# MLA attention: the queries' norm ahead of the up projection, first keys inside the queries' down projection, probabilities scaled on ScalarE

## The chip, the cores and the metric

One core of a Trainium2 chip runs the whole program. The metric is the device time of one execution in microseconds, the median of the runs shown; lower is better. The engines are named as in the profile: PE is TensorE's matrix multiplication (PEld its weight loads), DVE is VectorE, ACT is ScalarE, POOL is GpSimd, SP is the queue that issues most DMAs.

## The reference

The program is one step of a two-layer streaming encoder: a GLA layer and then an MLA layer, each between two half-step SwiGLU blocks, for 528 prompt rows (16 meta tokens and 512 frames) and 32 sample rows. The change lies in the MLA mixer:

```
def rmsnorm(x, w):
    y = x32 * lax.rsqrt(jnp.mean(x32 * x32, axis=-1, keepdims=True) + RMS_EPS)
    return (y * w.astype(jnp.float32)).astype(x.dtype)
...
cq, ckv, kr = jnp.split(xn @ w_down, [MLA_Q_RANK, MLA_Q_RANK + MLA_KV_RANK], axis=-1)   # 384, 256, 64
q = (rmsnorm(cq, q_norm) @ w_uq).reshape(B, L, MLA_HEADS, MLA_NOPE + MLA_ROPE)          # 8 heads, 128 + 64
q_rope = apply_rope(q[..., MLA_NOPE:], pos)
ckv = rmsnorm(ckv, kv_norm)
kr = apply_rope(kr[:, :, None, :], pos)[:, :, 0]
...
p = jax.nn.softmax(jnp.where(mask, s, -jnp.inf), axis=-1)      # per block of 128 queries
o = jnp.einsum('blhr,rhv->blhv', o_lat, w_uv).reshape(B, L, MLA_HEADS * MLA_V)
return o @ w_out, ckv, kr
```

The norm's factor, one number per row, commutes with the up projection `w_uq`; it may be multiplied in before or after it.

## The kernel before

All activations lie transposed: channels on the 128 partitions, rows along the free dimension (544 query columns: 512 frames and 32 sample rows; in two halves of 272, `HALF_Q`). Precision comes from splitting each fp32 operand into an upper part and a remainder: `split` writes the upper part with an ACT copy (line 374) and the remainder with a DVE subtraction (line 375), and every product is three matmuls, upper by upper (418), upper by weight remainder (419), remainder by upper (421) in `mm`, or 425 to 427 in `mm3`. Weights come in by DMA from SP (`load`, two raw buffers `raw`), and are split too (`whi`, `wlo`). PSUM holds three banks `ps` for projections and five banks `s` for scores, transposes and norms in this stage.

Code is written in pieces; a scheduler of the recording layer sets the order in which instructions stand in each engine's queue from the pieces' order and its own costs. Each engine then works off its queue strictly in order.

In `mla` the latent and rotary keys are projected first. Then come the queries: three blocks of 128 channels (`cq`) for the first half of columns, then three for the second half, each block 24 matmuls on `x`. Each block is multiplied by the input's norm (DVE, line 1158), by the norm's weights, and split (`cqh`, `cql`, lines 1160 and 1161); its squares are summed for the queries' own norm (`square`). `roots` sums the squares over partitions (three matmuls, line 450) and takes the inverse square root on DVE in three rounds of small operations (lines 485 to 493, tiles `rv`, `ry`, `rt`); its `finish` spreads the result over the partitions with three transposes (line 457). `query_norm` puts it into `yq` (line 1144) and scales cosine and sine by it on POOL (line 1146), so that the rotary part of the queries carries the norm without a further step; the plain part gets it after the up projection (line 1216), and is then split.

In `attention`, `keys(h)` makes a head's keys in two halves of 264 columns, `values(pr)` a head pair's values in five pieces, `queries(pr)` a pair's queries in six pieces: rotary, plain, plain for each half of the columns (nine matmuls each on `cqh`, `cql`; the rotary piece has four ACT copies, line 1013, a POOL product, line 1015, and four DVE steps behind it). `scores(h, t)` makes the scores of 128 queries against 144, 272, 400 or 528 keys and calls `softmax`: maximum on DVE (1027, 1030), exponential with a running sum on ACT (1032), reciprocal (1036) and scaling of the probabilities `p` (1038) on DVE. `transposes` turns the probabilities over on TensorE and splits them, `weigh` multiplies by the values. `weave(main, fill)` puts pieces of other work between the steps of a head. The order at the start was

```
for f in keys(0) + query_norm[:1] + keys(1) + query_norm[1:] + v0[:2] + queries(0):
    f()
weave([partial(scores, 0, t) for t in range(4)], v0[2:] + queries(1))
```

where `query_norm` holds `query_roots` and `query_norm` of the second half; those of the first half are called within the down projection of the second.

## Time and profile before

| | before |
|---|---|
| median of 3 runs | 2039.81 us (2038.86 to 2039.95) |
| profiled execution: time, span | 2041.99 us, 2040.2 us |
| granted TensorE clock, mean | 0.995 |
| PE, PEld busy | 2006.2 us (98%), 1976.2 us (97%) |
| DVE, ACT, POOL busy | 1603.3 us (79%), 1003.8 us (49%), 52.5 us (3%) |
| queries' down projection to the last head | about 1447 to 1630 us of the span |

The span runs from the first to the last instruction; the time also holds what lies around it. A busy share is an average over stages: what a change in one stage is worth is read from that stage, from what its engines wait for. A wait is put down to the release that came last. Matmuls overlap, so a group's mean duration is longer than the distance from one to the next.

### The profile page before, as it was taken

What the parts mean: (1) busy time and instruction counts of PE and PEld (TensorE: products, weight loads), DVE (VectorE), ACT (ScalarE), POOL (GpSimd) and SP (SyncE); (2) the same over time, 40 slices, a digit from 0 to 9 for tenths busy, and PEclk for the clock granted to TensorE, in tenths of its full rate; (3) what the DMA queues carried; (4) which work ended last, traced back from release to release, by engine and by line L of the source; (5) the groups of instructions that cost most, each with busy time, mean ns of one, the idle gap of its engine ahead of it and who ended that gap; (6) DMA issues with size and microseconds to landing.
All of it is one profiled execution on the core that took longest, in us unless ns stands there. A gap on an engine that the chain in (4) does not pass through costs nothing.

```text
span 2040.2 us, 38174 instructions
## 1 busy us (share of the span) xinstructions
PE 2006.2 (98%) x15408; PEld 1976.2 (97%) x15408; DVE 1603.3 (79%) x3046; ACT 1003.8 (49%) x1821; POOL 52.5 (3%) x121
## 2 busy tenths in 40 slices
PE   9999999999999999999999999999989999999997
PEld 8999999989999999999999999999989999999997
DVE  7778788556657988788888878786798898887884
ACT  6444445455535544444555444454476565444451
POOL 0000000101110000000000000000110000000000
PEclk9999999999999999999999999999999999999999
DMA  5232322212223132323313322323111413333221
GB/s 182 73 106 87 109 84 81 80 60 70 68 83 114 63 105 77 102 91 109 104 50 100 105 94 94 99 67 104 62 52 48 145 34 104 102 94 109 84 74 64
DMA packets 91904, 180.16 MB, mean 88 GB/s; under 512 B 10240, under 2 KB 21888, under 8 KB 91728
## 3 DMA queue, kind: packets, MB, share of 16 engines
q1 hardware_dynamic: 86688, 171.91, 26.6%
q10 hardware_dynamic: 5040, 5.82, 0.9%
q8 instruction: 121, 1.98, 0.4%
q14 instruction: 55, 0.45, 0.1%
HBM read 173.69 MB, written 3.99 MB: 87 GB/s over the span
## 4 chain that ended last, share of the span: by engine, by line
PE 81%; DVE 12%; ACT 3%; DMA 2%; issue 1%; POOL 0%; SPq 0%; DVEq 0%; ACTq 0%; POOLq 0%
PE Y L421 8%; PE Y L418 8%; PE Y L419 8%; PE A L418 5%; PE A L419 5%; PE A L421 5%; PE ps L418 4%; PE ps L421 4%; PE ps L419 3%; DVE wlo L375 3%; PE B L419 3%; PE B L421 3%; PE B L418 3%; PE C L421 3%; PE C L419 3%; PE C L418 3%
## 5 line engine op out<-in xcount | busy, mean ns | idle before, releaser
L418 PE MATMUL Y<-ah,whi 128*128 128x280 f32 (+1 forms) x1408 | 372.7, 291 | 3.2 <-ACT ah L374 2.4
L419 PE MATMUL Y<-ah,wlo 128*128 128x280 f32 (+1 forms) x1408 | 371.7, 290 | 0.0
L375 DVE TENSOR_TENSOR wlo<-fr,whi 128x1024 fp32r<-128x1024 f32 (+1 forms) x297 | 357.8, 1214 | 11.3 <-ACT whi L374 10.6
L374 ACT CAST whi<-fr 128x1024 fp32r<-128x1024 f32 (+1 forms) x297 | 308.5, 1048 | 103.4 <-PE C L421 39.6
L418 PE MATMUL A<-x,whi 128*128 128x280 f32 (+1 forms) x1056 | 281.8, 292 | 5.4 <-ACT whi L374 3.7
L419 PE MATMUL A<-x,wlo 128*128 128x280 f32 (+1 forms) x1056 | 281.2, 292 | 0.1
L418 PEld LDWEIGHTS Y<-ah,whi 128*128 128x128 f32 x1408 | 264.6, 188 | 4.5 <-ACT ah L374 3.3
L419 PEld LDWEIGHTS Y<-ah,wlo 128*128 128x128 f32 x1408 | 265.3, 188 | 0.0
L655 DVE SCALAR_TENSOR_TENSOR h<-Y,h 128x280 f32<-128x280 f32 (+1 forms) x320 | 141.1, 444 | 156.3 <-PE Y L421 155.8
L375 DVE TENSOR_TENSOR wlo<-raw,whi 128x512 fp32r<-128x512 f32 (+5 forms) x231 | 196.0, 850 | 78.9 <-ACT whi L374 74.1
L374 ACT CAST whi<-raw 128x512 fp32r<-128x512 f32 (+5 forms) x231 | 169.7, 736 | 163.4 <-PE ps L421 46.2
L421 PE MATMUL Y<-al,whi 128*128 128x280 f32 (+1 forms) x1408 | 232.7, 290 | 0.0
L293 DVE TENSOR_TENSOR fr<-fr 128x1024 f32<-128x1024 f32 x160 | 195.1, 1219 | 18.3 <-DMA fr<-W 15.7
L418 PEld LDWEIGHTS A<-x,whi 128*128 128x128 f32 x1056 | 199.9, 189 | 6.2 <-ACT whi L374 4.0
L419 PEld LDWEIGHTS A<-x,wlo 128*128 128x128 f32 x1056 | 199.9, 189 | 0.4 <-DVE wlo L375 0.4
L421 PEld LDWEIGHTS Y<-al,whi 128*128 128x128 f32 x1408 | 199.2, 188 | 0.0
L419 PE MATMUL B<-x,wlo 128*128 128x280 f32 (+1 forms) x704 | 186.4, 291 | 0.5 <-DVE wlo L375 0.5
L418 PE MATMUL B<-x,whi 128*128 128x280 f32 (+1 forms) x704 | 186.6, 291 | 0.0
L421 PE MATMUL A<-x,whi 128*128 128x280 f32 (+1 forms) x1056 | 178.9, 291 | 0.0
L418 PE MATMUL C<-x,whi 128*128 128x280 f32 (+1 forms) x672 | 177.5, 290 | 0.0
L419 PE MATMUL C<-x,wlo 128*128 128x280 f32 (+1 forms) x672 | 177.5, 290 | 0.0
L520 ACT COPY r<-A 128x560 f32<-128x560 f32 (+1 forms) x120 | 74.8, 623 | 159.2 <-PE A L421 158.4
(405 smaller groups left out, 4112.8 us busy)
## 6 DMA issues: line engine op xcount, KB each, us to landing
fr<-W SPq DMA_DIRECT2D x352, 256.0 KB, 3.4
raw<-W SPq DMA_DIRECT2D x80, 512.0 KB, 3.5
raw<-W SPq DMA_DIRECT2D x100, 256.0 KB, 2.9
raw<-W SPq DMA_DIRECT2D x40, 128.0 KB, 2.1
raw<-W SPq DMA_DIRECT2D x4, 384.0 KB, 3.1
h<-xT SPq DMA_DIRECT2D x2, 560.0 KB, 8.2
o_y<-h SPq DMA_DIRECT2D x8, 136.0 KB, 2.5
o_y<-h ACTq DMA_DIRECT2D x8, 136.0 KB, 2.3
```

Source lines behind the costliest of these rows:

```text
L293: self.net.nc.vector.tensor_tensor(r[out], r[x], r[y], op=ALU.add)
L374: self.nc.scalar.copy(hi, src)
L375: self.nc.vector.tensor_tensor(lo, src, hi.bitcast(F32), op=ALU.subtract)
L418: f(hi[:, b0 + k, :], xh[:, c], start=not more and k == 0, stop=False)
L419: f(lo[:, b0 + k, :], xh[:, c], start=False, stop=False)
L421: f(hi[:, b0 + k, :], xl[:, c], start=False, stop=k == n - 1)
L520: nc.scalar.copy(r[:, :, :n], of[:, :, :n])
L655: nc.vector.scalar_tensor_tensor(self.h[:, m, c], Y[:, :n], 0.5, self.h[:, m, c], op0=ALU.mult, op1=ALU.add)
```

## The change

The norm of the queries is multiplied in ahead of the up projection: `query_norm` reads the spread roots from PSUM, multiplies the three blocks of a half by them and by the weights (three DVE operations, line 1145 of the new code), and then splits all three blocks at once (a cast and a subtraction of 3 x 272 columns). The copies into `yq`, the scaling of cosine and sine and the sixteen products after the up projection go, and so do the scaled copy and the subtraction of each block (six of each); the plain pieces split their PSUM bank directly. The up projection of a half can now start only after that half's norm.

`keys` becomes a method, and the two halves of head 0's keys are put between the down projection's pieces for the second half of columns. Then come the first three pieces of head 0's and 1's queries, half of head 1's keys, the second half's norm, and the weave of head 0's scores with the remaining queries, keys and values. The pool of the down projection (`brief`) is closed after the norms, and the pool `at` (probabilities, values) is opened after that; its eight memsets on POOL move with it.

The scaling of the probabilities goes from a DVE operation to an ACT copy with a per-partition scale, 34 of them.

```
-        nc.vector.tensor_scalar(p[:, :n], p[:, :n], st[:, 5:6], None, op0=ALU.mult)
+        nc.scalar.activation(p[:, :n], p[:, :n], AF.Copy, scale=st[:, 5:6])
...
                 def query_norm(hf):
                     c = slice(*HALF_Q[hf])
-                    nc.scalar.copy(yq[:, c], norms.pop(hf)())
-                    for t in (self.cos, self.sin):
-                        nc.gpsimd.tensor_tensor(t[:, c], t[:, c], yq[:, c], op=ALU.mult)
+                    y = norms.pop(hf)()
+                    for m in range(3):
+                        nc.vector.scalar_tensor_tensor(cq[:, m, c], cq[:, m, c], nv[:, wq + m:wq + m + 1], y,
+                                                       op0=ALU.mult, op1=ALU.mult)
+                    self.split(cqh[:, :, c], cql[:, :, c], cq[:, :, c])
...
+                kt = {}
+                k0 = self.keys(two, kt, kph, kpl, 0)
                 for hf, (c0, c1) in enumerate(HALF_Q):
...
                         nc.vector.tensor_tensor(cq[:, m, c0:c1], Y[:, :n], xs.y[:, c0:c1], op=ALU.mult)
-                        w = nv[:, wq + m:wq + m + 1]
-                        nc.scalar.activation(cqh[:, m, c0:c1], cq[:, m, c0:c1], AF.Copy, scale=w)
-                        nc.vector.scalar_tensor_tensor(cql[:, m, c0:c1], cq[:, m, c0:c1], w,
-                                                       cqh[:, m, c0:c1].bitcast(F32), op0=ALU.mult, op1=ALU.subtract)
                         self.square(cq[:, m, c0:c1], n, hf, m == 0)
+                        if hf == 1 and m < 2:
+                            k0[m]()
...
-                qf = self.temp(("vh", "t")[j])
-                nc.vector.tensor_tensor(qf[:, :n], Y[:, :n], yq[:, c], op=ALU.mult)
-                self.split(q[h][0][:, c], q[h][1][:, c], qf[:, :n])
+                self.split(q[h][0][:, c], q[h][1][:, c], Y[:, :n])
...
+        q0, k1 = queries(0), keys(1)
+        for f in query_norm[:1] + q0[:3] + k1[:1] + query_norm[1:]:
+            f()
+        brief.close()
+        at = gone("at")
...
         v0 = values(0)
-        for f in keys(0) + query_norm[:1] + keys(1) + query_norm[1:] + v0[:2] + queries(0):
-            f()
-        weave([partial(scores, 0, t) for t in range(4)], v0[2:] + queries(1))
+        weave([partial(scores, 0, t) for t in range(4)], q0[3:] + k1[1:] + v0 + queries(1))
```

Three places in the engines' queues show what moved. First TensorE's queue around the transposes of the second half's norm (line 457; `ry` holds the roots, `cqh` and `cql` the parts of the queries' latent, `whi` and `wlo` those of a weight). Before, they stand within an up-projection piece:

```order
L419 MATMUL ps<-cqh,wlo 128x272
L421 MATMUL ps<-cql,whi 128x272
L457 MATMUL s<-ident,ry 128x128 x3
L421 MATMUL ps<-cql,whi 128x272 x2
L418 MATMUL ps<-cqh,whi 128x272
```

Now (`kpl` is the remainder of the latent keys, `kh` and `kl` are head 0's keys, `rph` and `rpl` the rotary keys, `x` here the queries):

```order
L421 MATMUL ps<-kpl,whi 128x264 x2
L457 MATMUL s<-ident,ry 128x128 x3
L425 MATMUL s<-kh,x 128x144
L426 MATMUL s<-kh,x 128x144
L427 MATMUL s<-kl,x 128x144
L1341 MATMUL s<-rph,x 128x144
L1342 MATMUL s<-rpl,x 128x144
```

The transposes moved from among the up projections to between head 1's first keys and head 0's first scores; the up projections of the second half stand behind those scores.

Second, VectorE's queue from the second half's sum of squares on (`rv`, `ry`, `rt` are the roots' small tiles; `acc`, `y`, `sq` belong to the rotary piece, `wlo` to a weight). Now:

```order
L485 TENSOR_SCALAR rv<-s 128x3
L486 TENSOR_SCALAR ry<-rv 128x3
L491 TENSOR_TENSOR rt<-ry 128x3
L1014 TENSOR_TENSOR acc<-ps,cos 128x272
L492 TENSOR_TENSOR rt<-rt,rv 128x3
L1017 TENSOR_TENSOR y<-acc,sq 64x272
L493 SCALAR_TENSOR_TENSOR ry<-rt,ry 128x3
L375 TENSOR_TENSOR wlo<-raw,whi 128x512
L491 TENSOR_TENSOR rt<-ry 128x3
L1018 TENSOR_TENSOR sq<-acc,sq 64x272
L492 TENSOR_TENSOR rt<-rt,rv 128x3
L1210 TENSOR_TENSOR x<-y,x 64x272
```

The rotary steps of the first queries moved in between the rounds of the root; before, splits of keys, values and weights stood there.

Third, ScalarE's queue at the load of the exponential's table (line 1032). Before:

```order
L374 CAST x<-t 128x272
L1207 CAST x<-sq 64x272
L374 CAST vh<-ps 128x256 x2
L1032 ACT_TABLE_LOAD
L1032 ACTIVATE p_17441,st<-s,st 128x144
```

Now:

```order
L374 CAST cqh<-cq 128x3x272
L1013 COPY sq<-ps 32x272
L1032 ACT_TABLE_LOAD
L1032 ACTIVATE p_17567,st<-s,st 128x144
L1013 COPY sq<-ps 32x272
L1038 ACTIVATE p_17567<-p_17567,st 128x144
L1013 COPY sq<-ps 32x272 x2
L374 CAST x<-ps 128x272 x2
```

The load and the first exponential moved in among the copies of the second half's rotary piece, ahead of the casts of that half's plain queries, and the scaling of the probabilities is new in this queue.

## The prediction

> **What bounds the kernel now.** I read the page's totals first, then the chain, then busy time by stretch in the MLA stage, then TensorE's own waits there.

> ```profile
> span 2040.2 us, 38174 instructions
> PE 2006.2 (98%) x15408; PEld 1976.2 (97%) x15408; DVE 1603.3 (79%) x3046; ACT 1003.8 (49%) x1821; POOL 52.5 (3%) x121
> PE 81%; DVE 12%; ACT 3%; DMA 2%; issue 1%; POOL 0%; SPq 0%; DVEq 0%; ACTq 0%; POOLq 0%
> ```

> TensorE is busy 98% of the span and carries 81% of the chain. The change removes no matmul, so it can only move TensorE's idle time, and only in the MLA stage. The view by stretch (span times, then busy time of each engine, clock last but two) shows where that idle time lies:

> ```profile
> core 0: us, PE busy (x) PEld busy (x) DVE busy (x) ACT busy (x) POOL busy (x), PEclk, DMA share, GB/s
> 1462.00:1476.00 14.00, 13.99 (x113) 13.55 (x112) 11.39 (x33) 8.12 (x21) 4.77 (x12) 1.00 0.28 82
> 1476.00:1494.00 18.00, 16.08 (x124) 15.43 (x122) 16.49 (x48) 14.12 (x36) 4.85 (x10) 1.00 0.21 63
> 1494.00:1510.00 16.00, 14.12 (x102) 12.84 (x101) 15.50 (x50) 11.95 (x33) 3.01 (x8) 1.00 0.03 9
> 1510.00:1530.00 20.00, 18.27 (x131) 16.57 (x130) 18.70 (x62) 15.85 (x47) 1.72 (x5) 1.00 0.23 66
> 1530.00:1562.00 32.00, 32.00 (x246) 31.06 (x246) 27.51 (x93) 19.16 (x61) 0.67 (x4) 1.00 0.24 73
> 1562.00:1600.00 38.00, 36.05 (x269) 34.53 (x267) 35.14 (x100) 26.12 (x68) 3.86 (x10) 1.00 0.26 77
> 1600.00:1645.00 45.00, 45.00 (x346) 43.98 (x346) 34.79 (x90) 22.43 (x52) 0.00 (x0) 1.00 0.35 115
> ```

> Length less PE busy gives 1.92, 1.88, 1.73, 0, 1.95 and 0 us from 1476 on: 7.5 us, 0.37% of the span, is all that there is to win. The stretches with idle time are those in which VectorE is busy 92 to 97%; at 86% (1530 to 1562) there is none. The longest waits name the same engine:

> ```profile
> PE ps L418 <- DVE vl L375: 1.8, 1, 1.8
> PE ps L418 <- DVE st L1030: 1.4, 1, 1.4
> PE s L425 <- DVE pTl L375: 0.9, 1, 0.9
> PE s L1274 <- ACT vh L374: 0.8, 1, 0.8
> ```

> **The change part by part.** Four places, walked through in TensorE's new order. These rows set the clock of the walk (start, duration, what):

> ```profile
> 1458.84 0.72 PE L450 MATMUL s<-ones,acc 128*128 128x1 f32 x6
> 1462.51 0.49 PE L457 MATMUL s<-ident,ry 128*128 128x128 f32 x3
> 1465.84 0.38 PE L1166 MATMUL s<-ident,cn 128*32 128x128 f32 x2
> 1466.79 0.29 PE L418 MATMUL ps<-kph,whi 128*128 128x264 f32 x1
> 1467.53 0.28 PE L418 MATMUL ps<-kph,whi 128*128 128x264 f32 x1
> 1468.38 0.80 PE L450 MATMUL s<-ones,acc 128*128 128x1 f32 x6
> 1469.21 0.16 DVE L485 TENSOR_SCALAR rv<-s 128x3 f32<-128x3 f32 x1 [0.30 <-PE s L450]
> 1473.57 0.51 PE L457 MATMUL s<-ident,ry 128*128 128x128 f32 x3
> 1474.17 0.29 PE L418 MATMUL ps<-cqh,whi 128*128 128x272 f32 x1
> 1475.31 0.29 PE L418 MATMUL ps<-cqh,whi 128*128 128x272 f32 x1
> ```

> Half a head's keys take 0.74 us (1466.79 to 1467.53), nine matmuls of a query piece 1.14 (1474.17 to 1475.31), roots plus one piece of the down projection 3.67 (1458.84 to 1462.51), transposes plus the next piece 3.33 (1462.51 to 1465.84). The rest comes from groups (busy us, mean ns of one, idle before):

> ```profile
> L1102 DVE SCALAR_TENSOR_TENSOR cn<-ck,nv,s 128x280 f32<-128x280 f32 x4 | 1.9, 504 | 0.0
> L375 DVE TENSOR_TENSOR kl<-ps,kh 128x264 fp32r<-128x264 f32 x16 | 6.6, 419 | 0.0
> L375 DVE TENSOR_TENSOR wlo<-raw,whi 128x768 fp32r<-128x768 f32 x4 | 3.8, 944 | 0.0
> L1216 DVE TENSOR_TENSOR vh<-ps,yn 128x272 f32<-128x272 f32 x8 | 3.4, 428 | 0.0
> L1038 DVE TENSOR_SCALAR p<-p,st 128x144 f32<-128x144 f32 (+3 forms) x32 | 12.5, 390 | 0.4
> L374 ACT CAST whi<-raw 128x1024 fp32r<-128x1024 f32 x12 | 12.6, 1051 | 4.1 <-PE ps L421 3.1 <-PE ps L426 0.8
> L1160 ACT ACTIVATE cqh<-cq,nv 128x272 fp32r<-128x272 f32 x6 | 3.1, 523 | 2.4 <-DVE cq L1158 2.4
> L1013 ACT COPY sq<-ps 32x272 f32<-32x272 f32 x32 | 12.1, 378 | 1.3 <-PE ps L421 0.8
> L1032 ACT ACTIVATE p<-s,st 128x144 f32<-128x144 f32 x8 | 3.1, 384 | 1.4 <-DVE st L1030 1.2
> L1032 ACT ACTIVATE p<-s,st 128x400 f32<-128x400 f32 x8 | 4.7, 593 | 4.2 <-DVE st L1030 4.2
> L1032 ACT ACT_TABLE_LOAD x1 | 1.3, 1283 | 0.0
> ```

> *First half's norm.* Head 0's keys (two halves) now stand between the pieces of the down projection, so TensorE has 0.74 + 3.09 us between roots and transposes and 0.74 + 3.08 between transposes and the first up projection. In the second gap stand VectorE's three multiplies (3 x 0.50), ScalarE's cast of 816 columns (0.87, scaled from 1.05 for 1024) and VectorE's subtraction of 816 (1.0, scaled from 0.94 for 768) with some 1.8 us of other work: the upper part is ready in time, the lower is needed only after six matmuls. Cost 0; without the keys as cover the lower part would come about 0.7 late (0.25 + 0.43 + 1.5 + 1.8 + 1.0, of which some 0.3 overlaps, against 3.08 + 0.14 + 0.75). The loads of the query weights go ahead of those of head 1's keys and the values on SP's queue; each piece still lands a buffer's turn before its split, cost 0. GpSimd's four scalings of cosine and sine go; its eight memsets now follow the first rotary product and are over before the first values are split, cost 0.

> *Second half's norm (a).* TensorE reaches the second transposes at 1458.84 + 3.67 + 0.74 + 3.33 + 0.74 + 0.14 + 3 x 1.14 + 0.62 (roots) + 0.74 = 1472.2. Its roots stand 0.74 + 13/9 x 1.14 + 0.62 ahead of that, at 1469.2; VectorE answers 0.83 us later, as at 1468.38 and 1469.21. There the square root's chain took 4.36 us up to the transposes (1469.21 to 1473.57) with six other operations in between. Now eight stand in between (seven of about 0.43, one of some 0.69, together 3.7 against 3.2): 4.9. The transposes start at 1474.9: a wait of 2.7 us where nine up-projection matmuls used to cover it. Between 0.3 (chain undisturbed) and 3.5 (rotary steps late).

> *Behind it (b, c).* Ten score matmuls (1.2 us) follow the transposes; meanwhile VectorE needs 0.25 + 3 x 0.50 and ScalarE 0.87 before the half-1 up projection may start: 0.3 + 2.6 - 1.5 gives b = 1.4. The lower part comes 1.0 after the cast, needed after six matmuls (0.75): c = 0.25.

> *Scores behind it (d).* Scores of queries 256 to 383 need the half-1 piece of head 0's queries, split by ScalarE behind a rotary copy (0.38), the table load (1.28), the first exponential (0.38), a copy, the first new scaling (0.42), two copies (0.76) and the cast itself (0.4): 4.0 us after the rotary piece, and 0.2 to begin. TensorE has 2.3 us of other up projection: d = 1.9, against 0.6 if the load fell into idle time. On the old queue the load stood behind value casts, with the scores not yet done.

> [...]

> ```profile
> 588.37 1.28 ACT L842 ACT_TABLE_LOAD   x1
> 589.66 0.67 ACT L842 ACTIVATE ab<-ab 128x560 f32<-128x560 f32 x1
> ```

> *ScalarE late with the next pair (e).* From the cast on ScalarE has some 9.8 us of queue before it frees the banks of the next pair's queries, TensorE 11.8 to get there; whether it also waits for TensorE on the way decides. Between 0 and 1.8 (the longest bank wait in the waits above); I take 1.0, the middle.

> *Probabilities and queries.* VectorE loses 34 scalings (0.39 each, 13 us) and 16 multiplies (0.43 each, 6.9). ScalarE gains 34 scalings. None like it is in the trace on p; 0.523 for 272 columns with a per-partition scale, and the exponentials' slope (0.209 over 256 columns), give 0.42 to 0.73, mean 0.575: 19.6 us. By stretch from 1494 (4, 6, 8 and 9 scalings, 4, 3, 0 and 4 multiplies) VectorE falls to 78, 76, 76 and 79%, ScalarE rises to 89, 96, 74 and 82%. Reading the idle time off today's stretches by the busier engine (86%: none; 92.5%: 5% of the stretch; 93.5%: 9%; 97%: 12%): 0.4, 2.1, 0 and 0, so 2.5 remain of 5.6. Ends 0 and 5.6.

> *Sum.* New waits 2.7 + 1.4 + 0.25 + 1.9 + 1.0 = 7.25, remaining 2.5, less the old 7.5: +2.25 us on a span of 2040.2. The profiled execution took 1.8 us beside its span and 2.2 more than the median of the three runs, 2039.81. Forecast: 2042.1, 0.1% longer. No change within 0.2% (4.1 us), about what a measurement of this kernel can tell, is 2035.7 to 2043.9.

> **The rivals.** *Faster.* The chain of the root runs undisturbed (a = 0.3 to 0.5), the table load falls into ScalarE's idle time (d = 0.6), and with VectorE below 80% no old wait survives: 0.5 + 1.4 + 0.25 + 0.6 - 7.5 = -4.75, 2035.1. For it speaks that at 86% VectorE costs nothing; against it that the eight operations and the load stand in the queues in that order. It needs a + d below about 1.7.

> *Slower: ScalarE takes VectorE's place.* From 1494 to 1530 its queue is 89 and 96% full, and each scaling waits in it for VectorE's reciprocal with casts behind it that free TensorE's banks. If the old 5.6 stays, the sum is 7.25 + 5.6 - 7.5 = +5.4, 2045.2. It decides from 4.4 us of remaining idle time on. For it: ScalarE's share there reaches what costs VectorE 9 to 12% today. Against: after 1530 it has a quarter free. [...]

> *No effect because the waits merely change place* is the forecast itself.

> **How the numbers follow.** Forecast case within 0.2%: 0.55, since a, b and d follow from fixed queues and they about equal what is saved. Slower 0.29: any 1.8 us more than my sum, from e or ScalarE's stretch. Faster 0.16. The low end, 2036.0, lets go some 0.15; the high end, 2046.5, is the forecast with the slower rival's 5.6 and a at 3.5 (2046.0), half a microsecond added; beyond it some 0.05.

> **What would show it.** Right: TensorE stops of 2 to 3 us ahead of the second query norm's transposes, 1 to 2 ahead of the half-1 up projection, about 2 ahead of the scores on ScalarE's cast of queries, and after them fewer waits on VectorE; ScalarE at 90% or more from 1494 to 1530. Wrong: transposes without a wait, or the total idle time from 1476 to 1645 below 4 or above 12 us.

## The result and the profile after

The changed kernel took 2053.16 us (median of 4 runs, 2048.41 to 2054.78) against 2039.88 of the kernel before beside it: ratio 1.0058, 95% interval 1.0046 to 1.0070. It is slower, by about 12 us as the ratio has it and 13.3 between the two medians; the forecast was 2042.1 with 2036.0 to 2046.5. The profiled execution took 2052.83 us with a span of 2051.0, 10.8 more than the span of before.

The page's totals of the kernel after:

```profile
span 2051.0 us, 38132 instructions
PE 2012.3 (98%) x15408; PEld 1982.7 (97%) x15408; DVE 1588.6 (77%) x2998; ACT 1017.0 (50%) x1849; POOL 49.0 (2%) x117
```

The same 15408 matmuls, and yet TensorE is busy 6.1 us longer. To place it, the next rows cut all kernels at the same two matmuls, one in the FFN ahead of the MLA stage (the 10501st) and one towards the stage's end (the 3150th from the last), so that the stretch holds the same work each time. Columns as in the view by stretch shown before; this is the kernel before:

```profile
1387.58:1629.56 241.98, 232.72 (x1761) 224.39 (x1759) 197.56 (x589) 142.20 (x371) 20.54 (x50) 1.00 0.25 80
```

And the kernel after:

```profile
1388.32:1637.22 248.90, 235.82 (x1760) 227.04 (x1758) 183.03 (x541) 155.59 (x399) 17.02 (x46) 0.99 0.24 78
```

The stage is 6.92 us longer. Length less PE busy is the idle time: 13.08 against 9.26, so 3.82 more. The other 3.10 is busy time above 232.72: the same matmuls at a granted clock that was not always 1.00 (0.99 in the mean here, last column but two). From here on "idle" and "clock price" of a kernel mean these two numbers, taken from its own row. VectorE lost 14.5 us of work and ScalarE gained 13.4, as the change wants, and it did not help.

Of the rest, 0.74 lies ahead of the stretch, 0.19 in the 340 us behind it, and 2.99 in the tail, whose code the change does not touch. The tail before and after, from the same matmul to the end:

```profile
1969.86:2040.20 70.34, 57.74 (x452) 56.23 (x450) 37.62 (x88) 16.55 (x30) 0.00 (x0) 0.95 0.25 77
```

```profile
1977.71:2051.04 73.33, 59.60 (x452) 57.99 (x450) 38.05 (x88) 16.55 (x30) 0.00 (x0) 0.91 0.24 74
```

Of that, 1.86 is busy time again, at a lower clock (PEclk 0.95 and 0.91); the other 1.13 is idle time. So 4.96 of TensorE's 6.1 us are found. By stretch within the stage, the kernel after:

```profile
core 0: us, PE busy (x) PEld busy (x) DVE busy (x) ACT busy (x) POOL busy (x), PEclk, DMA share, GB/s
1462.00:1476.00 14.00, 11.64 (x93) 11.23 (x91) 11.62 (x37) 7.22 (x17) 1.25 (x5) 1.00 0.22 68
1476.00:1494.00 18.00, 14.88 (x92) 14.02 (x93) 11.48 (x34) 10.09 (x25) 3.99 (x11) 0.81 0.07 22
1494.00:1510.00 16.00, 14.39 (x109) 13.45 (x108) 13.04 (x39) 14.62 (x41) 3.06 (x8) 1.00 0.18 59
1510.00:1530.00 20.00, 19.78 (x140) 18.69 (x141) 16.79 (x54) 18.20 (x50) 2.85 (x6) 1.00 0.16 47
1530.00:1562.00 32.00, 30.54 (x235) 29.46 (x235) 26.41 (x87) 23.73 (x71) 0.67 (x4) 1.00 0.24 73
1562.00:1600.00 38.00, 35.77 (x265) 33.73 (x264) 29.18 (x82) 28.21 (x74) 3.56 (x10) 1.00 0.24 72
```

The idle time sits at the stops of TensorE's timeline (start, duration, instruction, and in brackets the idle time ahead of it and what ended it):

```profile
1476.84 0.51 PE L457 MATMUL s<-ident,ry 128*128 128x128 f32 x3 [3.20 <-DVE ry L493]
...
1479.66 0.60 PE L418 MATMUL ps<-cqh,whi 128*128 128x272 f32 x1 [0.95 <-ACT cqh L374]
...
1487.02 0.58 PE L425 MATMUL s<-kh,x 128*128 128x400 f32 x2 [1.32 <-ACT x L374]
...
1497.97 0.39 PE L418 MATMUL ps<-cqh,whi 128*128 128x272 f32 x1 [0.28 <-DVE acc L1014]
...
1501.08 0.39 PE L418 MATMUL ps<-cqh,whi 128*128 128x272 f32 x1 [1.08 <-DVE x L375]
...
1534.31 0.55 PE L1274 MATMUL s<-ident,psm 128*128 128x128 f32 x3 [1.46 <-ACT psm L1038]
...
1575.70 0.39 PE L418 MATMUL ps<-cqh,whi 128*128 128x272 f32 x1 [0.84 <-DVE x L375]
```

The first three are the forecast's a, b and d. What no term had is behind the first: four stretches of 3.41 us, cut where the clock changed:

```profile
1474.78:1478.19 3.41, 1.35 (x12) 1.38 (x13) 2.97 (x11) 0.64 (x3) 0.00 (x0) 1.00 0.36 120
1478.19:1481.60 3.41, 2.46 (x11) 2.14 (x11) 2.48 (x9) 0.87 (x1) 0.84 (x4) 0.50 0.00 0
1481.60:1485.02 3.42, 3.42 (x17) 3.42 (x16) 0.04 (x1) 2.18 (x5) 0.01 (x1) 0.50 0.00 0
1485.02:1488.43 3.41, 2.09 (x16) 1.88 (x16) 1.88 (x6) 3.35 (x11) 1.54 (x5) 1.00 0.00 0
```

A stretch with 1.35 of 3.41 us busy is followed by two at half clock (0.50).

### The profile page after: what moved, and what is told of

It reads as the page before. It is cut to its first block, busy times and chain, and to the rows that moved or that the text cites. A ratio compares the mean times of both kernels' runs of the same rounds, so it can differ in the third digit from the quotient of the medians.

```text
span 2051.0 us, 38132 instructions
## 1 busy us (share of the span) xinstructions
PE 2012.3 (98%) x15408; PEld 1982.7 (97%) x15408; DVE 1588.6 (77%) x2998; ACT 1017.0 (50%) x1849; POOL 49.0 (2%) x117
## 5 line engine op out<-in xcount | busy, mean ns | idle before, releaser
L418 PE MATMUL Y<-ah,whi 128*128 128x280 f32 (+1 forms) x1408 | 374.7, 292 | 4.1 <-ACT ah L374 3.2
L375 DVE TENSOR_TENSOR wlo<-fr,whi 128x1024 fp32r<-128x1024 f32 (+1 forms) x297 | 357.7, 1214 | 11.3 <-ACT whi L374 11.1
L374 ACT CAST whi<-fr 128x1024 fp32r<-128x1024 f32 (+1 forms) x297 | 308.5, 1047 | 103.7 <-PE C L421 37.6
L418 PE MATMUL A<-x,whi 128*128 128x280 f32 (+1 forms) x1056 | 281.3, 292 | 5.6 <-ACT whi L374 3.9
L418 PEld LDWEIGHTS Y<-ah,whi 128*128 128x128 f32 x1408 | 266.2, 189 | 5.5 <-ACT ah L374 4.3
L375 DVE TENSOR_TENSOR wlo<-raw,whi 128x512 fp32r<-128x512 f32 (+5 forms) x231 | 195.7, 849 | 81.6 <-ACT whi L374 76.8
L374 ACT CAST whi<-raw 128x512 fp32r<-128x512 f32 (+5 forms) x231 | 169.7, 736 | 165.1 <-PE ps L421 44.8
L421 PE MATMUL Y<-al,whi 128*128 128x280 f32 (+1 forms) x1408 | 234.2, 292 | 0.0
L418 PEld LDWEIGHTS A<-x,whi 128*128 128x128 f32 x1056 | 199.4, 189 | 6.4 <-ACT whi L374 4.2
L421 PEld LDWEIGHTS Y<-al,whi 128*128 128x128 f32 x1408 | 201.5, 189 | 0.0
L418 PE MATMUL B<-x,whi 128*128 128x280 f32 (+1 forms) x704 | 187.0, 291 | 0.0
L421 PE MATMUL A<-x,whi 128*128 128x280 f32 (+1 forms) x1056 | 178.8, 291 | 0.0
L418 PE MATMUL C<-x,whi 128*128 128x280 f32 (+1 forms) x672 | 177.3, 290 | 0.0
```

Source lines behind the costliest of these rows:

```text
L374: self.nc.scalar.copy(hi, src)
L375: self.nc.vector.tensor_tensor(lo, src, hi.bitcast(F32), op=ALU.subtract)
L418: f(hi[:, b0 + k, :], xh[:, c], start=not more and k == 0, stop=False)
L421: f(hi[:, b0 + k, :], xl[:, c], start=False, stop=k == n - 1)
```

## The experiments

All in one table; "idle" and "clock price" as above, in us (a clock price between -0.5 and 0.9 also arises between kernels whose clock stayed at 1.00). Both are read from one execution of each kernel; in the kernel before, e10 and e12, which the ratio does not tell apart, the idle time is 9.26, 9.36 and 9.60. The kernel before ran beside each group of kernels, with medians from 2039.88 to 2042.59; so kernels of different groups are compared by their ratios. The rows stand with the runs on which the argument rests.

| kernel | median us | ratio to before, 95% interval | idle | clock price |
|---|---|---|---|---|
| before | 2039.88 | | 9.26 | 0 |
| after | 2053.16 | 1.0058 (1.0046 to 1.0070) | 13.08 | 3.10 |
| e1 | 2051.93 | 1.0060 (1.0046 to 1.0075) | 15.13 | 2.62 |
| e2 | 2045.23 | 1.0022 (1.0013 to 1.0031) | 10.64 | 1.47 |
| e3 | 2047.57 | 1.0036 (1.0024 to 1.0048) | 12.42 | 3.40 |
| e4 | 2053.44 | 1.0065 (1.0052 to 1.0078) | 12.36 | 7.08, with 20 matmuls more |
| e5 | 2051.47 | 1.0047 (1.0029 to 1.0066) | 10.95 | 4.98, with 24 matmuls more |
| e6 | 2050.89 | 1.0048 (1.0029 to 1.0066) | 13.86 | 3.54 |
| e7 | 2049.68 | 1.0041 (1.0027 to 1.0055) | 12.82 | 0.69 |
| e8 | 2047.54 | 1.0029 (1.0019 to 1.0039) | 12.25 | 2.32 |
| e9 | 2048.07 | 1.0031 (1.0021 to 1.0042) | 12.12 | 0.94 |
| e10 | 2042.79 | 1.0005 (0.9996 to 1.0013) | 9.36 | 0.63 |
| e11 | 2044.46 | 1.0011 (1.0003 to 1.0020) | 12.18 | -0.45 |
| e12 | 2042.32 | 1.0007 (0.9997 to 1.0017) | 9.60 | -0.16 |
| e13 | 2048.47 | 1.0037 (1.0023 to 1.0051) | 12.35 | 3.49 |
| e14 | 2046.16 | 1.0022 (1.0014 to 1.0031) | 11.89 | 1.23 |
| e15 | 2043.28 | 1.0012 (1.0001 to 1.0024) | 10.44 | -0.03 |
| e16 | 2044.46 | 1.0016 (1.0007 to 1.0024) | 12.39 | -0.30 |
| e17 | 2040.04 | 0.9990 (0.9981 to 0.9999) | 9.56 | -0.32 |
| e18 | 2050.59 | 1.0038 (1.0025 to 1.0050) | 13.96 | 3.34 |

### The scalings on ScalarE (e1, e2, e14)

e1, in the kernel after; e2 is the opposite edit in the kernel before, e14 the same line there with `nc.gpsimd`:

```
-        nc.scalar.activation(p[:, :n], p[:, :n], AF.Copy, scale=st[:, 5:6])
+        nc.vector.tensor_scalar(p[:, :n], p[:, :n], st[:, 5:6], None, op0=ALU.mult)
```

> The changed kernel with one part undone: the 34 scalings of the probabilities are on VectorE again (0.39 us each), all else as changed. Theory W (the stop ahead of the second query norm's transposes, 3.2 us, with 0.95 behind it and some 3.0 of TensorE at half clock after it, is the loss; the scalings are not): the stop and the half clock at about 1478 stay, idle time after 1494 moves by no more than 2 us either way, time 2051 to 2055 us. Rival S (the scalings on ScalarE are the loss: they hold up its casts from 1494 on, 5.9 us of idle there): most of that 5.9 goes, at least 4 us faster than the changed kernel, below 2049.

Measured 2051.93: theory W by its time, and the rival S falls. W's bound on the idle time after 1494 is missed upwards, 8.2 us up to 1645 in place of 5.8; over the whole stretch it is 2.05 more without the scalings on ScalarE.

> The kernel before with this one part of the change alone: the scalings of the probabilities on ScalarE. Theory W: VectorE is relieved by 13 us where it is 92 to 97% busy and ScalarE was at most 79% busy, so the 7.5 us of idle time in the stage shrinks by 1 to 4: 2036 to 2039 us, no half clock in the stage. Rival S: idle time from 1494 on grows by 4 us or more: 2044 us or more.

Measured 2045.23: the time that S wanted, but not by its 4 us of idle time. So the scalings alone do harm in the kernel before: 1.4 us more idle time and 1.5 of clock, after a stretch that was 1.61 of 3.41 us busy:

```profile
1477.93:1481.34 3.41, 1.61 (x13) 1.35 (x13) 3.24 (x12) 2.65 (x6) 2.11 (x5) 1.00 0.01 2
1481.34:1484.75 3.41, 3.41 (x15) 3.40 (x14) 2.43 (x9) 2.15 (x8) 0.00 (x0) 0.50 0.38 100
```

The stage explains 2.9 of the 4.7 us between the medians. VectorE is busy 10.0 us less in the stretch, and that won nothing.

> The kernel before with the 34 scalings of the probabilities on GpSimd, which is 3% busy, in place of VectorE; nothing else changed. If VectorE's load (92 to 97% from 1476 to 1530) is what keeps TensorE idle 7.5 us and the scalings only have to leave it without filling ScalarE: 1 to 4 us faster than before, 2037 to 2040. If the delay of the probabilities counts (a product of 128x272 takes GpSimd 0.77 us against 0.43 on VectorE): the transposes of probabilities wait, 2042 or more.

Measured 2046.16: slower too. The group of the scalings on GpSimd:

```profile
L1038 POOL TENSOR_SCALAR p<-p,st 128x144 f32<-128x144 f32 (+3 forms) x32 | 36.6, 1142 | 80.9 <-DVE st L1036 51.3 <-DVE x L375 9.0 <-PE s L427 5.0
```

1142 ns against 390 on VectorE, and one stop of 2.9 us on it. In the kernel before both other engines cost time, though each unloads VectorE; that the delay of the probabilities is what costs is shown for GpSimd by that stop, for ScalarE only argued.

### The second half's norm: stop and clock (e3, e4, e5)

e3 gives the second half its norm behind the up projection again (scaled copy and subtraction per block, copy into `yq`, product on VectorE), and leaves the rest:

```
+                    if hf == 1:
+                        nc.scalar.copy(yq[:, c], norms.pop(hf)())
+                        for t in (self.cos, self.sin):
+                            nc.gpsimd.tensor_tensor(t[:, c], t[:, c], yq[:, c], op=ALU.mult)
+                        return
...
+                if c0:
+                    qf = self.temp(("vh", "t")[j])
+                    nc.vector.tensor_tensor(qf[:, :n], Y[:, :n], self.yq[:, c], op=ALU.mult)
```

> The changed kernel, but the second half of the queries gets its norm as in the kernel before, after its up projection (scaled copies and subtractions of each block, copy into yq, products on VectorE, cosine and sine scaled on GpSimd); the first half's norm ahead, the keys in the down projection, the new order and the scalings on ScalarE stay. Nine more up-projection matmuls and some can then go ahead of the second transposes. Theory W: the stop of 3.2 us and the 0.95 behind it go, the clock stays at 1.00 between 1476 and 1494, some 7 us less than the changed kernel: 2044 to 2048 us. Rival S: the time stays within 2 us of the changed kernel's 2053.2.

Measured 2047.57, in W's range, but not by W's reason: the stop of 3.20 is gone (0.3 is left), and other stops leave 12.42 idle, with the clock down twice (PEclk 0.88 between 1462 and 1476, 0.91 between 1476 and 1494). Of the 13.3 us between the medians 7.1 are left.

e4 and e5 fill the stop with matmuls whose results nobody reads, e4 in a bank of the projections, e5 in one of the scores (24 in place of 20):

```
+        def idle():
+            Y = self.bank("s")
+            for _ in range(24):
+                pe.matmul(Y[:, :272], kph[:, 0, :P], cqs[0][0][:, :272], start=True, stop=True)
...
-        for f in query_norm[:1] + q0[:3] + k1[:1] + query_norm[1:]:
+        for f in query_norm[:1] + q0[:3] + k1[:1] + [idle] + query_norm[1:]:
```

> The changed kernel with 20 matmuls of 128x272 whose results nobody reads (about 2.5 us) ahead of the second query norm's transposes, where TensorE stood idle for 3.2 us. It tells the wait from the clock. If the clock fell because TensorE stood idle (theory W): VectorE's chain is as late as before, the transposes start at the same time, but the granted clock stays at 1.00 after it, and some 3 us are saved: 2049 to 2051 us. If the half clock had another cause: it stays, and the time stays at 2052 to 2054. Rival S expects no change either way, 2053.

Measured 2053.44. The filling waited for its bank, 1.96 us, and the half clock came all the same (1.45 of 3.41 us busy, then PEclk 0.50 from 1476.44), so this does not tell the wait from the clock:

```profile
1476.15 4.30 PE L1423 MATMUL ps<-cqh,kph 128*128 128x272 f32 x20 [1.96 <-DVE kl L375]
```

> As the fill before it (unread matmuls ahead of the second transposes of the changed kernel), but 24 of them (about 3.0 us) in one of the five banks of the scores: with a bank of the projections the filling matmuls themselves stood still for 2.0 us until VectorE had freed it, so TensorE was idle all the same and the clock fell. Theory W: now TensorE is busy from 1473.4 to 1476.4, the transposes start when they did, the clock stays at 1.00 between 1476 and 1486, some 3 us saved: 2049 to 2051.5. If the half clock has another cause than the idle time: 2052 to 2055 with a granted clock of 0.5 at about 1478.

Measured 2051.47. Now the transposes start at 1476.38 after 0.15 idle, and the clock stays at 1.00 until the next stop, of the scores on ScalarE's cast, which has grown from 1.32 to 2.40 us because TensorE gets there at full clock:

```profile
1481.92:1485.33 3.41, 1.01 (x9) 0.79 (x7) 0.69 (x3) 3.31 (x9) 0.41 (x1) 1.00 0.00 0
1485.33:1488.74 3.41, 3.41 (x16) 3.41 (x17) 3.02 (x8) 2.61 (x8) 1.74 (x6) 0.50 0.00 0
```

So the half clock at 1478 came from the stop and goes with it, and the next stop brings it back: filling one hands it on. Measured against the kernel before beside it e5 is 10.0 us slower, where the kernel after was 13.3, with intervals that overlap; the time is just inside W's range.

### Work as cover, the table, and everything together (e6, e7, e8)

```
+            Y = self.bank("s" if h == 1 and c0 else "ps")          # keys
+                Y = self.bank("s" if pr == 0 and i < 2 else "ps")  # values
...
-        for f in query_norm[:1] + q0[:3] + k1[:1] + query_norm[1:]:
+        for f in query_norm[:1] + q0[:3] + k1 + v0[:2] + query_norm[1:]:
```

> The changed kernel with useful work in the stop: the second half of head 1's keys and two pieces of values (about 2.1 us of TensorE, in banks of the scores) go ahead of the second norm's transposes; the values' tiles get their place early. No work is added. Theory W: the stop of 3.2 us shrinks to about 1.1, the clock stays at 1.00 after it, and behind the transposes the up projection waits longer (0.95 becomes about 1.8, since VectorE has the splits of the values first): 3.2 - 1.1 - 0.9 + 3.0 = 4.2 us less than the changed kernel, 2047 to 2051. Rival S: within 1.5 us of 2053.

Measured 2050.89. The stop is 1.07 now, but the up projection waits 1.69 in place of 0.95 and the scores 2.40 in place of 1.32; idle 13.86. The waits change place. Its clock price belongs to an earlier place (PEclk 0.83 between 1441.5 and 1462), as in e8 and e13 below.

e7 adds one exponential after the first half's down projection, so that the table is loaded there; e8 also puts the scalings back on VectorE:

```
+                        if hf == 0 and m == 2:
+                            warm = kp.tile([P, 2], F32, name="warm")
+                            nc.scalar.activation(warm[:, :1], cq[:, 2, :1], AF.Exp, scale=0.0)
```

> The kernel with the cover, and the exponential's table loaded early: one exponential of a 128x1 tile after the first half's down projection, where ScalarE has idle time, so that the load of 1.28 us is gone from the queue ahead of the casts of the half-1 queries. The wait of the scores of queries 256 to 383 on ScalarE's cast (1.3 us in the changed kernel) falls to 0.6 or less: 0.5 to 1.3 us faster than the cover alone. If that wait is set by something else than the load, no difference.

Measured 2049.68, with the wait on the cast down from 2.40 to 1.1 us, about the load's 1.28, and not to the 0.6 expected. The whole gain against e6 cannot be told from none (the intervals overlap). Here the clock stays at 1.00 through the whole stretch, and the stage is 4.25 longer than before, 3.56 of it idle time:

```profile
1386.85:1633.08 246.23, 233.41 (x1761) 224.61 (x1759) 182.68 (x541) 155.91 (x400) 15.80 (x44) 1.00 0.25 78
```

> The kernel with cover and early table, and the scalings of the probabilities on VectorE again. Rival S: 4 us or more faster than with them on ScalarE, since they delay the softmaxes and the casts behind them. Theory W: within 2 us of it. This is the candidate to come near the kernel before: if cover, table and scalings are all that was lost, 2038 to 2043; if the order of the first scores itself costs (wait on the second half's norm and the queries right ahead of the scores), 2045 or more.

Measured 2047.54, 2.1 less than e7, just outside W's 2 and far from S's 4, with intervals that overlap. Its clock price lies at the start of the stage (PEclk 0.83 between 1441.5 and 1462). With cover, early table and the scalings back it is still 6.0 us slower than before: about half of the loss is none of these.

### The place of the scores (e9, e10, e13)

e9, in the kernel after:

```
-        for f in query_norm[:1] + q0[:3] + k1[:1] + query_norm[1:]:
+        for f in query_norm[:1] + q0[:3] + k1 + query_norm[1:]:
...
-        weave([partial(scores, 0, t) for t in range(4)], q0[3:] + k1[1:] + v0 + queries(1))
+        for f in v0[:2] + q0[3:]:
+            f()
+        weave([partial(scores, 0, t) for t in range(4)], v0[2:] + queries(1))
```

> The changed kernel with the place of the scores undone: both halves of head 1's keys ahead of the second norm, behind it two pieces of values and the half-1 queries, and only then head 0's scores, woven with the other values and the next queries as before. Norm ahead and scalings on ScalarE stay. If the scores behind half the queries are the loss (theory O: softmax work on ScalarE and VectorE stands between the norm and the half-1 queries' splits, and each stop hands on to the next): the waits of scores on ScalarE's casts (1.3 to 2.4 us) and of the up projection go, 4 us or more faster than the changed kernel, below 2049. If the norm's chain ahead of the up projection is the loss wherever the scores stand (theory N): the stop ahead of the transposes (2.5 us) stays and the loss with it, 2050 to 2054.

Measured 2048.07, below O's 2049, and N's stop ahead of the transposes is down to 0.2. In its place TensorE waits 2.0 us for a split of keys and 1.5 for another split; the clock stays at 1.00, but 12.12 idle remain.

```profile
1385.69:1631.47 245.78, 233.66 (x1760) 224.63 (x1758) 183.21 (x541) 155.55 (x399) 15.54 (x46) 1.00 0.25 78
```

e10 moves only the half-1 queries of head 0 and 1 into the weave of the kernel before (`v0[:2] + q0[:3]` ahead, `q0[3:] + v0[2:] + queries(1)` within).

> The kernel before with one part of the change alone: head 0's scores woven behind half of the queries (the three half-0 pieces ahead, the half-1 pieces within the weave). Norm behind the up projection, scalings on VectorE. Theory O: slower than before by 2 us or more, 2043 or above, by waits of scores on casts of queries. Theory N: within 2 us of before.

Measured 2042.79, not told from before, idle 9.36. The new place of the scores costs nothing that can be told by itself; in the changed kernel undoing it helped (e9).

e13 is e9 with the early table and the scalings on VectorE.

> What stays of the change when the scalings go back to VectorE and the scores back behind all queries: the norm ahead of the up projection for both halves and the first keys in the down projection (with the exponential's table loaded early, which by itself told no difference in the kernel before). Theory A (the parts add up: scalings on ScalarE 4.7 us as measured on the kernel before, first half's norm and keys 2.2, place of the scores 5.4 on top): 2041 + 1 to 3, so 2042 to 2045 us. Theory N (the second half's norm ahead costs by itself, some 2.5 us of stop and the half clock behind it, wherever the scores stand): 2046 or more.

Measured 2048.47; theory A falls, idle 12.35 again. The time is N's, its mechanism is not: no stop ahead of the transposes is left in the list of waits, and the half clock lies at the start of the MLA stage, where the code is that of before, so that the clock price of 3.49 is not the change's.

```profile
1437.60:1441.01 3.41, 2.26 (x19) 2.04 (x18) 2.01 (x11) 1.36 (x4) 0.00 (x0) 1.00 0.17 54
1441.01:1447.84 6.83, 6.83 (x33) 6.82 (x32) 4.11 (x23) 2.77 (x7) 0.78 (x1) 0.50 0.00 1
```

The longest waits are on the subtraction of queries (`x`, line 375), which frees a bank of the projections, and on that of keys. The first of them comes back below:

```profile
PE ps L418 <- DVE x L375: 4.0, 4, 1.7
PE ps L418 <- DVE kl L375: 1.9, 1, 1.9
```

### The first half's norm, costed at nothing (e11, e12, e15, e16)

e11 is e3 with the scalings on VectorE and the order of keys, values, queries and scores as before: what is left of the change is the first half's norm ahead and the first keys in the down projection. e15 keeps of these only the keys' place, e16 only the norm (all three, and e17 below, keep the later opening of the pool `at`). e12 is the kernel before with the early table.

> The kernel before with only the first half's norm ahead of its up projection and the first keys in the down projection; second half's norm, order of keys, values, queries and scores, and the scalings on VectorE as before. VectorE has eight products of 272 columns less (3.4 us) where it is over 90% busy. Theory N and O: this keeps the part of the change without a chain on TensorE's path, so it is no slower than before and up to 2 us faster: 2037 to 2041. If the keys in the down projection are what costs (they take the cover of the first transposes of keys(0) away from the second norm): 2043 or more.

Measured 2044.46, idle 12.18: 2.9 us more idle time from the part that N and O held for harmless. The time is the one named for the keys' place, 2043 or more; e15 and e16 separate the two.

> The kernel before with the exponential's table loaded early (one exponential of a 128x1 tile after the first half's down projection). The load of 1.28 us stood in ScalarE's queue ahead of the first exponential, behind which TensorE waited up to 1.8 us for banks. If it was on the path: 0.5 to 1.3 us faster than before. If not: no difference that can be told.

Measured 2042.32, idle 9.60: no difference that can be told. The load was not on the path there.

> The kernel before with only the place of head 0's keys changed: their two halves stand between the down projection's pieces of the second half; both norms behind the up projection, scalings on VectorE, scores as before. The kernel with this and the first half's norm ahead had 2.9 us more idle time of TensorE in the stage (12.2 against 9.3 from the same first to the same last matmul). Theory K (the keys' 1.5 us of TensorE work go to where TensorE was never idle, and are missing as cover where VectorE is over 90% busy): idle 10.5 to 12.5 in the stage, 1 to 3 us slower than before. Theory F (the first half's norm ahead is what costs): idle within 0.7 of 9.3, no difference.

Measured 2043.28, 2.4 slower by the ratio as theory K wanted, idle 10.44 and so just short of K's 10.5. The 1.2 us are two stops at the keys' new place (start, duration, instruction, idle time ahead):

```profile
1472.68 0.80 PE L450 MATMUL s<-ones,acc 128*128 128x1 f32 x6 [0.64 <-DVE acc L440]
...
1474.07 0.38 PE L425 MATMUL ps<-whi,kph 128*128 128x256 f32 x1 [0.59 <-DVE kl L375]
```

So the keys' place costs something when it stands alone; neither stop is there in the kernel after.

> The kernel before with only the first half's norm ahead of its up projection, head 0's keys at their old place behind the down projection. VectorE has 3.4 us less to do in the products after the up projection, and a cast of 816 columns on ScalarE and one product and subtraction more at once. Theory K: idle within 0.7 of 9.3 or less, 0 to 1 us faster than before. Theory F: idle 10.5 to 12.5, 1 to 3 us slower.

Measured 2044.46 and theory F: one half's norm ahead leaves 3.1 us more idle time than before, where the whole change leaves 3.8. The parts do not add up: keys' place and norm together (e11) have 2.9.

```profile
1390.59:1635.40 244.81, 232.42 (x1760) 224.29 (x1758) 195.45 (x582) 142.18 (x368) 19.53 (x48) 1.00 0.25 79
```

VectorE has 2.1 us less to do in this stretch. Its list of TensorE's waits names something that before did not have, the banks of the projections (`ps`) waiting for the subtraction of queries (`x`, line 375), and the scores waiting for softmaxes:

```profile
PE ps L418 <- DVE x L375: 2.2, 3, 1.1
PE s L425 <- ACT p L1032: 1.7, 2, 1.3
PE ps L418 <- DVE t L1227: 1.4, 2, 1.0
```

### The bank (e17, e18)

With the norm behind, one VectorE product (0.43 us, line 1216 of before) read the PSUM bank and freed it; the split then ran from SBUF. With the norm ahead the split reads the bank: ScalarE's cast (0.38 in the kernel after), then VectorE's subtraction behind it (0.43), and only then is it free; the up projection waited on that subtraction for 2.4 us in the kernel after and 2.2 in e16. There are three such banks. e17 is e16, e18 the kernel after, with a copy put in:

```
-                self.split(q[h][0][:, c], q[h][1][:, c], Y[:, :n])
+                qf = self.temp(("vh", "t")[j])
+                nc.vector.tensor_copy(qf[:, :n], Y[:, :n])
+                self.split(q[h][0][:, c], q[h][1][:, c], qf[:, :n])
```

> The kernel before with the first half's norm ahead alone, as in the run before, but its plain queries are first copied on VectorE from their PSUM bank to SBUF and split from there, as the product did before; eight copies of 128x272 (about 0.43 us each) more work for VectorE. Theory B (the bank: with the norm ahead the split reads PSUM directly, so a bank comes free only after ScalarE's cast and VectorE's subtraction, one behind the other, where one product freed it; with three banks TensorE waits on it): waits of the up projection on VectorE's subtraction of queries (2.2 us) go, idle time in the stage falls from 12.4 to 9.3 to 10.5, 1 to 3 us faster although work is added. Theory V (VectorE's load): idle 12.4 or more, same time or slower.

Measured 2040.04, 0.9990 (0.9981 to 0.9999) of before, where e16 stood at 1.0016, with eight VectorE operations more than e16.

```profile
1386.48:1628.44 241.96, 232.40 (x1760) 224.25 (x1758) 197.27 (x590) 141.86 (x368) 18.70 (x48) 1.00 0.25 80
```

Idle is 9.56, and the wait on line 375 of `x` is gone from its list:

```profile
PE ps L418 <- DVE vl L375: 1.7, 1, 1.7
PE ps L418 <- DVE st L1030: 1.4, 1, 1.4
PE s L425 <- DVE pTl L375: 0.9, 1, 0.9
PE s L1289 <- ACT vh L374: 0.8, 1, 0.8
```

These are nearly the waits of the kernel before. Theory B holds for this half: less idle time with more work on VectorE. The scheduler also ordered VectorE's queue differently around the copies, and the two effects are not separated. Against before the stretch is as long as it was (241.96 and 241.98), so the 0.1% by which e17 beats it cannot be placed.

> The changed kernel with the same copy for all 16 plain pieces (6.9 us more for VectorE). Theory B: the waits of the up projection on the subtraction of queries (2.4 us in the changed kernel) go, idle time in the stage 10.5 to 12 (13.1 in the changed kernel), 1 to 3 us faster than its 2053.2. Theory V: idle 13 or more, the same or slower.

Measured 2050.59: the time that theory B wanted, with an interval that just overlaps that of the kernel after, and the idle time that V wanted, 13.96. The waits on `x` are gone here as well, others have come, and the stop ahead of the transposes stands:

```profile
PE s L457 <- DVE ry L493: 3.1, 2, 2.8
PE s L425 <- DVE pTl L375: 1.5, 1, 1.5
PE ps L418 <- ACT cqh L374: 1.3, 1, 1.3
```

Its stretch is 1.1 us longer than that of the kernel after, in an execution that took 2048.78 us; where the lower time comes from is not shown. With the second half's norm in the way, taking these waits off did not lower the idle time.

## Why the prediction was wrong, by its own steps

*The premise.* "The change removes no matmul, so it can only move TensorE's idle time, and only in the MLA stage." This step failed. Of the 10.84 us by which the profiled execution grew, 3.82 are idle time in the stage, where the sum had 2.25. 3.10 in the stage and 1.86 in the tail are the same matmuls at a lower granted clock, for which the sum has no term, and the remaining 2.06 lie outside the stage and stay unexplained. The quoted rows of before showed clock 1.00 throughout the stage, with 1.80 us as the longest stop; the forecast put one of 2.7 there and did not ask what it does to the clock. The fill e5 shows that the stop of 3.20 brought the half clock behind it.

The clock alone did not put the result outside the range, though. 2053.16 less 4.96 is 2048.2, and the range ended at 2046.5. Over all the runs its part is smaller: the mean granted clock was 0.9928 in the four runs of the kernel after and 0.9948 in the 17 of the kernel before beside e1. An estimate from these two, their difference of 0.0020 times the span, is about 4 us at most: it takes TensorE as busy all through the half clock.

*First half's norm, "Cost 0".* This step failed too. It checked whether the norm would be ready in time, which it was (no stop of TensorE between 1450 and 1473.6), and not what the plain queries' split straight from PSUM does to the banks: 3.1 us of idle time with that half alone (e16), 2.8 of it given back by a copy (e17). The 16 multiplies that VectorE loses were counted as a gain; each had also freed a bank.

*Probabilities and queries, 2.5 remaining.* This step failed as a method. Its busy shares came out within some 8 points: in the four stretches from 1494 ScalarE is at 91, 91, 74 and 74%, where 89, 96, 74 and 82 were forecast, VectorE at 82, 84, 83 and 77 for 78, 76, 76 and 79. The idle time read from them did not: 1.61, 0.22, 1.46 and 2.23 us in place of 0.4, 2.1, 0 and 0. From 1494 to 1600 that is 5.5 us, 1.36 of them e's; 4.2 stand against the 2.5. The stretches of the kernel before did not even lie on one curve: from 1476 to 1494 VectorE was busy 92% and TensorE idle 11%, more than the 5% read at 92.5, and that stretch was left out. e2 and e14 show it from the other side: VectorE relieved, idle time up. The forecast's slower rival named the scalings on ScalarE as the cause; taking them back in the changed kernel gained nothing that can be told (e1).

*Second half's norm (a) and behind it (b).* Right in place, 2.7 forecast and 3.20 measured, 1.4 and 0.95. That the sum came out, 4.1 and 4.15, is partly luck, since the two misses cancel. The eight operations between the root's steps took the 3.7 us forecast, but the chain from the first step to the transposes took 5.71 in place of 4.9. Most of the difference is one step of 128x3, which took 0.72 us in place of 0.15, while GpSimd's rotary product ran; that one held the other is not shown:

```profile
1471.45 0.78 POOL L1015 TENSOR_TENSOR sq<-sq,sin 128x272 f32<-128x272 f32 x1 [19.81 <-ACT sq L1013]
...
1471.53 0.72 DVE L491 TENSOR_TENSOR rt<-ry 128x3 f32<-128x3 f32 x1
```

*Scores behind it (d).* 1.9 forecast, 1.32 measured, ScalarE's cast as named. At half clock (0.50 from 1478.19 to 1485.02) TensorE came later and so waited less; at full clock (e5) it is 2.40. Without the load (e7 against e6) it is 1.3 less. Beside the load's 1.28 us the queue shows no further time: the copy ahead ends 0.01 us before it (1482.79 and 0.38), the exponential starts 0.02 us behind it:

```profile
1482.79 0.38 ACT L1013 COPY sq<-ps 32x272 f32<-32x272 f32 x1 [3.18 <-PE ps L421]
1483.18 1.28 ACT L1032 ACT_TABLE_LOAD   x1
1484.48 0.38 ACT L1032 ACTIVATE p<-s,st 128x144 f32<-128x144 f32 x1
```

*ScalarE late with the next pair (e).* 1.0 forecast; 0.28 and 1.08 measured at that place, but VectorE's subtraction ended the longer one and not a late ScalarE: a bank held by two operations.

*The signs.* None of those named for being wrong showed: the transposes waited, and the idle time from 1476 to 1645 was 8.9 us, between the 4 and 12 set for it. They looked at idle time alone, and so missed the clock.

Still open: which part of the change's idle time is the first half's norm and which the second's in the changed kernel itself, where the copy did not help (e18); why the scalings cost 4.7 us on the kernel before (the stage shows 2.9); and how much of the change's 12 us is the tail's clock, which a profile of one execution cannot tell.

## What to carry to other kernels

The products that read the PSUM banks here did two things, their arithmetic and the release: with the first half's norm ahead, and so without eight of them, TensorE stood idle 3.1 us longer (e16), and with copies in their place 2.8 of that was gone (e17). Before such an operation is taken away, ask what will read the bank last and how many engines stand in line for that. Give every forecast stop a second price: where TensorE was busy for 1.01 to 1.61 us of a stretch of 3.41, the traces read here show the next 3.41 or 6.83 us at half clock (0.50), and filling that stop handed the price to the next one (e5). A busy share tells how full an engine is, not whether TensorE waits for it: work moved from a VectorE at 92 to 97% to a less busy ScalarE or GpSimd lost time here (e2 and e14, both 1.0022 of before).

## What was not expected of the hardware

```profile
1480.29:1483.70 3.41, 1.67 (x15) 1.42 (x13) 3.21 (x10) 3.19 (x7) 2.23 (x6) 1.00 0.01 2
1483.70:1487.11 3.41, 3.41 (x25) 3.41 (x26) 3.37 (x15) 1.84 (x7) 0.00 (x0) 1.00 0.23 59
```

```profile
1478.79:1482.20 3.41, 1.79 (x13) 1.41 (x13) 3.18 (x10) 2.65 (x6) 0.42 (x2) 1.00 0.12 41
1482.20:1485.61 3.41, 3.41 (x15) 3.39 (x15) 2.30 (x10) 3.25 (x10) 1.11 (x4) 0.50 0.01 2
```

At the start of the stage 2.26 us in e13 were followed by half clock (0.50) as well. What decides there is not shown.

The time of one program moved with its clock: among 34 runs of the kernel before beside e9 to e12 it went from 2036.53 us at a mean granted clock of 0.997 to 2047.30 at 0.991. That the place of the grid is the reason is likely, but not shown.
